# Fixing the order of TensorE's work around the first way back of a long convolution

## The chip, the cores and the metric

The kernel runs on one core of a Trainium2 chip, in float32. The metric is the device time of one execution in microseconds. A core has TensorE (PE, matmuls), VectorE (DVE), ScalarE (ACT), GpSimd (POOL) and SyncE (SP), each with its own queue that is worked off in order, and 16 DMA engines that are shared by the transfers which SP, ACT and POOL issue.

## The reference

One layer of an encoder over 1024 positions and 1024 channels: a normalised input `xn` is multiplied by one large matrix `w_in`, whose columns feed a state-space branch (S5), a long-convolution branch (Hyena), their gates and the merge. What matters here is the Hyena branch:

```python
proj = xn @ w_in[l]
u_s5, g_s5, p_hy, g_hy, m_logits = jnp.split(proj, SPLITS, axis=-1)
...
v, x1, x2 = jnp.split(sc, HY_ORDER + 1, axis=-1)      # sc: width-3 convolution of p_hy
kf = hyena_filters(L, w1, b1, freq, w2, b2, w3, decay)
z = v.astype(f32)
for o, g in enumerate((x1, x2)):
    zf = jnp.fft.rfft(z, n=2 * L, axis=1)
    conv = jnp.fft.irfft(zf * kf[:, o][None], n=2 * L, axis=1)[:, :L]
    z = g.astype(f32) * (conv + d[o].astype(f32) * z)
return z.astype(proj.dtype) * jax.nn.silu(gate)
```

So `z` goes to frequencies and back twice. The first way back is multiplied by the gate `x1`, the second by `x2` and by the SiLU of a further projection.

## The kernel before

Every product is computed with operands split in a high and a low part, in three passes (high x high, high x low, low x high). A **projection** is one call of `proj`: 128 output channels over all positions, 3 x 8 x 2 = 48 matmuls into a PSUM tile `pps` (there are two), whose rows are all L541. Its weights come in by `prefetch`, in the fixed order of `self.order`: a load by SP into `wraw` (L508, three buffers), ACT's cast to `whi` (L510) and negation into `wlo` (L511), and an adding transfer issued by POOL that leaves the residue in `wlo` (L512). There are two pairs of `whi` and `wlo` (`wp`, two buffers), so weights are at most two projections ahead.

The stages around the change, in order of the program:

- `hy_forward0`: the first way to the frequencies. Projections of v are turned and multiplied with the constants `zc` (L686, L697); DVE combines the results with the filter's spectra (L704 to L725) and ACT stores the spectra to DRAM (L761).
- `hy_inverse0`: the first **way back**, eight blocks of 128 channels. `inverse` multiplies four spectra (`yraw`, loaded by SP at L609 and split into `y` by ACT and DVE, L109 and L113) with the constants `ic` (eight loads by SP, L600, into the space that the first forward stage has left): 48 matmuls, L633 and L635. ACT and DVE join the halves (L639 to L644), POOL multiplies by the gate and writes the sums over the gate's tile (`rotate`, L821 to L825). `store` then **turns** the block by eight transposes (L671), splits it into `z1`, which has a single buffer (L673, L674), and ACT sends it to DRAM (L831). The gates come from eight projections of x1 (`use_x1`); there are five gate tiles, so the gate of x1(5) can be written only after block 0 has been turned.
- `hy_forward1`: the second way to the frequencies, like the first, from the blocks stored in DRAM. Beside it run 16 projections, in pairs gate(c) and x2(c): ACT takes the SiLU of gate(c) into the single tile `sg` (L871), and x2(c) is convolved (L563 to L566), folded with it (L589 to L591) and stored (L878).
- `tail` and `output`: the second way back (`hy_inverse1`, the same `inverse`), whose pools and constants are set up when the second forward stage is closed, then the two last matrices.

The order on each engine is fixed before the kernel runs, by a scheduler: of the instructions whose inputs are ready by its own reckoning it queues the earliest in program order. So a projection that stands later in the program is pulled forward where the PE would otherwise have nothing. `tc.issue_after(i)` sets a bound to that: whatever is traced in its block on the engine of `i` is queued behind `i`. In the kernel before there are two such places here: x2(2) stands behind the last turn, and the second forward stage behind x2(2).

Of the kernel before, what the change touches and what calls it, by code (L numbers as in the profile page):

```python
# [9 lines left out]
F = mybir.dt.float32  # L10
# [7 lines left out]
L = 1024  # L18
# [82 lines left out]
class Trunk:  # L101
# [422 lines left out]
    def proj(self, c, use, name="w_in", x=None):  # L524

        self.projs([(c, use)], name, x or (self.xh, self.xl), ())

    def projs(self, cols, name, x, cuts):

        nc = self.nc  # L530
        xh, xl = x
        nk = xh.shape[1]
        part = lambda x, kc, hf: x[kc, hf] if x is self.xl else x[:, kc, hf * 512:hf * 512 + 512]
        todo = [(self.weight((name, c, nk)), self.pp.tile([128, L], F, name="pps"), use) for c, use in cols]
        for a, b in zip((0,) + cuts, cuts + (nk,)):
            for (hi, lo), ps, _ in todo:
                for p in range(3):
                    for kc in range(a, b):
                        w, x = ((hi, xh), (hi, xl), (lo, xh))[p]
                        for hf in range(2):  # L540
                            self.summed = nc.tensor.matmul(  # L541
                                             out=ps[:, hf * 512:hf * 512 + 512], lhsT=w[:, kc], rhs=part(x, kc, hf),
                                             start=a == 0 and p == 0 and kc == 0, stop=b == nk and p == 2 and kc == nk - 1)
        for _, ps, use in todo:
            use(ps)
# [69 lines left out]
    def inverse(self, pi):  # L615

        nc = self.nc
        ps = pi.tile([128, 2, 512], F, name="iv")
        for nj, j in enumerate((0, 2, 1, 3)):
            while len(self.iv_ready) < self.iv_ahead and self.iv_todo:  # L620
                self.spectrum()
            y = self.iv_ready.pop(0)
            for par in range(2):
                for pqi in range(2):
                    cols, dst = (((slice(0, 258), ps[:, 0, 0:258]), (slice(514, 770), ps[:, 0, 256:512])),
                                 ((slice(258, 514), ps[:, 1, 0:256]),
                                  (slice(770, 1026), ps[:, 1, 256:512])))[par][pqi]
                    for a, b in ((0, 0), (0, 1), (1, 0)):
                        lhsT = y[:, a, par, pqi]
                        first = nj == 0 and pqi == 0 and a == 0 and b == 0  # L630
                        last = nj == 3 and pqi == 1 and a == 1
                        if first and par == 0:
                            nc.tensor.matmul(out=ps[:, 0], lhsT=lhsT, rhs=self.ic0, start=True, stop=False)  # L633
                        else:
                            nc.tensor.matmul(out=dst, lhsT=lhsT, rhs=self.ic[b][:, j, cols], start=first, stop=last)  # L635
        while len(self.iv_ready) < self.iv_ahead and self.iv_todo:
            self.spectrum()
        s = self.iv_w.tile([128, 2, 256], F, name="isn", bufs=1)
        nc.scalar.copy(out=s, in_=ps[:, :, 256:512])  # L639
        pm = self.iv_w.tile([128, 2, 512], F, name="pm")  # L640
        for a, op in enumerate((ALU.add, ALU.subtract)):
            nc.vector.tensor_tensor(out=pm[:, a].rearrange("p (b q) -> p b q", b=2), in0=ps[:, :, 0:256], in1=s, op=op)
        nc.vector.tensor_copy(out=pm[:, 0, 0:1], in_=ps[:, 0, 0:1])
        nc.vector.tensor_copy(out=pm[:, 1, 0:1], in_=s[:, 0, 0:1])  # L644
        return pm
# [18 lines left out]
    def to_time(self, pt, eo, z):  # L664

        nc = self.nc
        for h in range(2):
            ps = pt.tile([128, 4, 128], F, name="zt", tag="fw")
            for b in range(4):
                c = (4 * h + b) * 128  # L670
                self.turned = nc.tensor.transpose(out=ps[:, b], in_=eo[:, c:c + 128], identity=self.ident)  # L671
            hi, lo = (z[:, i, 4 * h:4 * h + 4] for i in range(2))
            nc.scalar.copy(out=hi, in_=ps)  # L673
            nc.vector.tensor_tensor(out=lo, in0=ps, in1=hi, op=ALU.subtract)  # L674
# [131 lines left out]
    def hy_inverse0(self):  # L806

        tc, nc = self.tc, self.nc
        self.d_z1 = self.dram.tile([4, 128, 2, 2048], F, name="d_z1")
        with ExitStack() as ctx:  # L810
            self.inv_pools(ctx, 0, (4, 4))
            zp = ctx.enter_context(tc.tile_pool(reuse_waits="tile", name="iv_z", bufs=1, side="right"))
            pi = ctx.enter_context(tc.tile_pool(reuse_waits="tile", name="iv_p", bufs=1, space=PSUM, side="right"))
            pt = ctx.enter_context(tc.tile_pool(reuse_waits="tile", name="iv_pt", bufs=2, space=PSUM, side="right"))
            gates, back = {}, {}
            self.inverse_start(0)

            def rotate(c):
                g = gates.pop(c)
                pm = self.inverse(pi)  # L820
                nc.gpsimd.tensor_tensor(out=pm, in0=pm, in1=g, op=ALU.mult)  # L821
                nc.gpsimd.tensor_tensor(out=g[:, 0], in0=pm[:, 0], in1=pm[:, 1], op=ALU.add)
                nc.gpsimd.tensor_tensor(out=g[:, 1], in0=pm[:, 0], in1=pm[:, 1], op=ALU.subtract)
                nc.gpsimd.tensor_copy(out=g[:, 0, 0:1], in_=pm[:, 0, 0:1])
                nc.gpsimd.tensor_scalar(out=g[:, 1, 0:1], in0=pm[:, 1, 0:1], scalar1=-1.0, scalar2=None, op0=ALU.mult)  # L825
                back[c] = g

            def store(c):
                z = zp.tile([128, 2, 8, 128], R, name="z1")
                self.to_time(pt, back.pop(c).rearrange("p a b -> p (a b)"), z)  # L830
                nc.scalar.dma_start(out=self.d_z1[c // 2][:, c % 2], in_=z.rearrange("p h a c -> p (h a c)").bitcast(F))  # L831

            for c in range(10):
                def use_x1(ps):
                    g = self.gates[c % len(self.gates)]
                    self.fold(self.conv(ps, 8 + c, "cv"), None, g)
                    gates[c] = g.rearrange("p a b c d -> p a (b c d)")

                if c < 8:
                    self.proj(16 + c, use_x1)  # L840
                if 0 < c < 9:
                    rotate(c - 1)
                if c > 1:
                    store(c - 2)

    def hy_forward1(self, tail):

# [2 lines left out]
        with self.tc.tile_pool(reuse_waits="tile", name="sg", bufs=1) as sp, self.tc.tile_pool(reuse_waits="tile", name="vf1", bufs=2) as self.vf, \  # L850
                ExitStack() as ctx:
            wp, fwd = self.fwd_pools(ctx, 1)

            def forwards():
                for cq in range(4):
                    z = wp.tile([128, 2, 2, 8, 128], R, name="z")
                    for ct in range(2):
                        nc.sync.dma_start(out=z[:, ct].rearrange("p h a c -> p (h a c)").bitcast(F),
                                          in_=self.d_z1[cq][:, ct])
                    yield  # L860
                    yield from fwd(cq, z)

            f = forwards()
            next(f)
            silu = {}

            def gate(c):
                silu[c] = sp.tile([128, L], F, name="sg")

                def use_g(ps):  # L870
                    nc.scalar.activation(out=silu[c], in_=ps, func=AF.Silu)  # L871
                self.proj(32 + c, use_g)

            def x2(c):
                def use_x2(ps):
                    t = self.vf.tile([128, 2, 2, 2, 128], F, name="vf")
                    self.fold(self.conv(ps, 16 + c, "cv"), silu.pop(c), t)
                    nc.scalar.dma_start(out=self.d_x2[c], in_=t.rearrange("p a b c d -> p (a b c d)"))  # L878
                self.proj(24 + c, use_x2)

            blocks = [(use, c) for c in range(8) for use in (gate, x2)]
            for use, c in blocks[:5]:
                use(c)
            with self.tc.issue_after(self.turned.ins):
                x2(2)
            with self.tc.issue_after(self.summed.ins):
                next(f)
            for _ in f:
                pass
            ctx.close()  # L890
            tail()
            for use, c in blocks[6:]:
                use(c)

    def exp(self, pool, out, x, shape):

# [598 lines left out]
```

## Time and profile before

| | us |
|---|---|
| median of three runs | 1426.94 (1425.91 to 1428.88) |
| profiled execution | 1429.46 |
| its span | 1427.5 |
| PE busy | 1352.0 |
| DVE busy | 1011.3 |
| ACT, POOL busy | 515.6, 385.3 |

The profile is of one execution. Its timeline names start and length of each run of like instructions, and in brackets how long the engine had been idle and what ended that. Matmul lengths overlap their successors, so the pace of a run of matmuls is read from one start to the next. The table of stretches gives each engine's busy time in it and PEclk, the clock granted to TensorE, 1.00 being 2.4 GHz and 0.50 being 1.2 GHz.

### The profile page before, as it was taken

The numbers are of one execution on the slowest core, as the hardware profiler recorded it, in microseconds if no ns is written. First come the engines' busy times: TensorE is split into PE (matmuls) and PEld (weight loads), VectorE is DVE, ScalarE is ACT, GpSimd is POOL, SyncE is SP. The second block draws the span as 40 slices with busy tenths as digits, with TensorE's granted clock in tenths as the row PEclk, the third lists the DMA queues.
The fourth block names the chain that finished last, engine by engine and source line by source line (L and its number), as shares of the span: only waits on it lengthen the run. The fifth ranks groups of instructions, "written<-read, shape, count | busy, mean of one in ns | idle before, by whom it ended". The sixth has DMA issues, their size and how long they took to land.

```text
span 1427.5 us, 19526 instructions
## 1 busy us (share of the span) xinstructions
PE 1352.0 (95%) x7219; PEld 1138.5 (80%) x7219; DVE 1011.3 (71%) x1938; ACT 515.6 (36%) x737; POOL 385.3 (27%) x331
## 2 busy tenths in 40 slices
PE   5888899999999999999999999999799998999998
PEld 3777788888887877878888888888688877978886
DVE  7999998699589887314389995455388966843632
ACT  5576664223333232333233223443222224432322
POOL 3766775000000000232122200335301112332222
PEclk9998999999999999999999999999899997999999
DMA  8221224865685554566975659765878899766431
GB/s 278 84 83 74 82 97 144 203 164 143 178 275 140 117 125 94 151 165 173 324 218 169 175 178 270 204 193 187 287 248 270 261 299 301 204 186 153 132 108 71
DMA packets 188619, 257.24 MB, mean 180 GB/s; under 512 B 23069, under 2 KB 144153, under 8 KB 185788
## 3 DMA queue, kind: packets, MB, share of 16 engines
q1 hardware_dynamic: 149212, 153.69, 34.6%
q0 software_dynamic: 11520, 39.85, 14.5%
q10 hardware_dynamic: 27792, 62.45, 12.1%
q8 instruction: 57, 0.93, 0.3%
q14 instruction: 38, 0.31, 0.1%
HBM read 147.49 MB, written 76.82 MB: 157 GB/s over the span
## 4 chain that ended last, share of the span: by engine, by line
PE 61%; DVE 15%; DMA 9%; issue 3%; SPq 1%; ACT 1%; DVEq 0%; ACTq 0%
PE pps L541 38%; PE ops L1396 6%; PE iv L635 6%; DMA d_y<-x 3%; PE po L404 2%; PE fwo L686 2%; PE pe L414 1%; DMA d_z<-z 1%; DMA wlo<-wraw 1%; DMA yraw<-d_y 1%; DMA zc<-c_zc_lo_d 1%; DVE st L1228 1%; DVE st L1226 1%; PE zt L671 1%; DVE m L722 1%
## 5 line engine op out<-in xcount | busy, mean ns | idle before, releaser
L512 POOL DMA_DIRECT2D wlo<-wraw x76 | 65.9, 867 | 683.5 <-ACT wlo L511 509.1
L541 PE MATMUL pps<-xh,whi 128*128 128x512 f32 x896 | 227.4, 402 | 9.9 <-ACT sg L871 6.7
L541 PE MATMUL pps<-xl,whi 128*128 128x512 f32 x896 | 225.0, 397 | 0.0
L541 PE MATMUL pps<-xh,wlo 128*128 128x512 f32 x896 | 221.9, 396 | 0.0
L541 PEld LDWEIGHTS pps<-xh,whi 128*128 128x128 f32 x896 | 168.3, 191 | 49.0 <-ACT sg L871 6.9
L541 PEld LDWEIGHTS pps<-xh,wlo 128*128 128x128 f32 x896 | 166.9, 188 | 39.1
L541 PEld LDWEIGHTS pps<-xl,whi 128*128 128x128 f32 x896 | 165.9, 188 | 38.0 <-issue 0.2
L510 ACT CAST whi<-wraw 128x1024 fp32r<-128x1024 f32 (+1 forms) x76 | 74.7, 983 | 286.1 <-PE pps L541 266.9
L404 PE MATMUL po<-sh,fo 128*128 128x256 f32 x512 | 100.8, 291 | 6.2 <-DVE sh L111 5.1
L113 DVE TENSOR_TENSOR y<-yraw,y 128x512 fp32r<-128x512 f32 x64 | 55.0, 873 | 71.1 <-ACT y L109 70.8
L635 PE MATMUL iv<-ic,y 128*128 128x256 f32 (+1 forms) x752 | 99.0, 290 | 5.2 <-ACT y L109 3.2
L635 PEld LDWEIGHTS iv<-ic,y 128*128 128x128 f32 x752 | 97.2, 198 | 8.0 <-ACT y L109 3.7
L404 PEld LDWEIGHTS po<-sh,fo 128*128 128x128 f32 x512 | 83.7, 196 | 9.1 <-DVE sh L111 6.1
L511 ACT ACTIVATE wlo<-whi 128x1024 fp32r<-128x1024 f32 (+1 forms) x76 | 74.9, 986 | 27.3 <-PE pps L541 25.5
L357 POOL TENSOR_TENSOR acc<-acc,sq 128x512 f32<-128x512 f32 x56 | 76.8, 1371 | 22.2 <-ACT sq L342 20.1
L404 PE MATMUL po<-sl,fo 128*128 128x256 f32 x256 | 74.0, 289 | 1.0 <-DVE sl L113 1.0
L109 ACT CAST y<-yraw 128x512 fp32r<-128x512 f32 x64 | 39.1, 621 | 62.5 <-PE iv L635 43.9
L404 PEld LDWEIGHTS po<-sl,fo 128*128 128x128 f32 x256 | 50.2, 196 | 2.1 <-DVE sl L113 1.3
L564 DVE SCALAR_TENSOR_TENSOR cv<-pps,cw,cv 128x1023 f32<-128x1023 f32 x24 | 30.7, 1278 | 28.7 <-ACT cv L563 28.7
L333 PE MATMUL g<-w3h,ha 128*128 128x512 f32 x64 | 33.6, 525 | 17.1 <-DVE e L338 16.1
L686 PE MATMUL fwo<-z,zc 128*128 128x256 f32 x384 | 49.6, 283 | 0.0
L336 ACT ACTIVATE e<-dec,negt 128x512 f32<-128x512 f32 x64 | 45.2, 716 | 11.5 <-DVE so L350 4.8
(437 smaller groups left out, 2674.6 us busy)
## 6 DMA issues: line engine op xcount, KB each, us to landing
wlo<-wraw POOLq DMA_DIRECT2D x64, 512.0 KB, 5.7
wraw<-w_in SPq DMA_DIRECT2D x56, 512.0 KB, 5.2
kspec<-ko SPq DMA_DIRECT2D x32, 512.0 KB, 3.0
kt<-kspec SPq DMA_DIRECT2D x32, 512.0 KB, 4.9
d_y<-x ACTq DMA_DIRECT2D x32, 512.0 KB, 3.6
yraw<-d_y SPq DMA_DIRECT2D x64, 256.0 KB, 5.5
d_m<-cv ACTq DMA_DIRECT2D x16, 512.0 KB, 2.7
d_z<-z ACTq DMA_DIRECT2D x8, 1024.0 KB, 4.5
```

Source lines behind the costliest of these rows:

```text
L109: nc.scalar.copy(out=hi, in_=src)
L113: e.tensor_tensor(out=lo, in0=src, in1=hi, op=ALU.subtract)
L336: nc.scalar.activation(out=e, in_=decf, func=AF.Exp, scale=negt[:, tt:tt + 1])
L357: nc.gpsimd.tensor_tensor(out=acc, in0=acc, in1=sq, op=ALU.add)
L404: nc.tensor.matmul(out=po[:, part], lhsT=fo[a][:, 12 * (jj % 2) + b], rhs=sd[4 + i][d][:, part], start=n == 0 and part == 0, stop=n == 11 ...
L510: nc.scalar.copy(out=hi, in_=raw)
L511: nc.scalar.activation(out=lo, in_=hi, func=AF.Copy, scale=-1.0)
L512: nc.gpsimd.dma_start(out=lo, in_=raw, accum_op=ALU.add)
L541: self.summed = nc.tensor.matmul(out=ps[:, hf * 512:hf * 512 + 512], lhsT=w[:, kc], rhs=part(x, kc, hf), start=a == 0 and p == 0 and kc == ...
L635: nc.tensor.matmul(out=dst, lhsT=lhsT, rhs=self.ic[b][:, j, cols], start=first, stop=last)
L686: nc.tensor.matmul(out=out, lhsT=zc[a][:, b], rhs=z[:, :, d, zi], start=start and n == 0, stop=stop and n == 3 * len(prods) - 1)
L1396: nc.tensor.matmul(out=pss[cs.start][:, 0:cs.stop - cs.start], lhsT=m[:, kc, ts], rhs=w[kc][:, cs], start=kc == 0 and p == 0, stop=kc == 7 ...
```

## The change

The x1 projections of the first way back are divided: five come whole ahead of block 0, the other three are cut into their three passes (`proj_thirds`), and one or two such thirds are put between two blocks, by the list 1, 2, 1, 1, 1, 2, 1, 0. On the PE every block is queued behind the third before it, every third behind the block before it. Only gate(0) is then bound between the last block and the second forward stage; the other 15 late projections follow in the program after the second forward stage and after `tail`, in the order x2(0), gate(1), x2(1) and on, with no bound.

```diff
+    def proj_thirds(self, c, use):
+
+        nc = self.nc
+        (hi, lo), ps = self.weight(("w_in", c, 8)), self.pp.tile([128, L], F, name="pps")
+        for p, (w, x) in enumerate(((hi, self.xh), (hi, None), (lo, self.xh))):
+            for kc in range(8):
+                for hf in range(2):
+                    cs = slice(hf * 512, hf * 512 + 512)
+                    self.summed = nc.tensor.matmul(out=ps[:, cs], lhsT=w[:, kc],
+                                                   rhs=self.xl[kc, hf] if x is None else x[:, kc, cs],
+                                                   start=p == 0 and kc == 0, stop=p == 2 and kc == 7)
+            if p == 2:
+                use(ps)
+            yield
...
-            for c in range(10):
+            def x1(c):
                 def use_x1(ps):
...
-                if c < 8:
-                    self.proj(16 + c, use_x1)
-                if 0 < c < 9:
-                    rotate(c - 1)
-                if c > 1:
-                    store(c - 2)
+                return 16 + c, use_x1
+
+            for c in range(5):
+                self.proj(*x1(c))
+            thirds = (t for c in range(5, 8) for t in self.proj_thirds(*x1(c)))
+            for c, n in enumerate((1, 2, 1, 1, 1, 2, 1, 0)):
+                with tc.issue_after(self.summed.ins):
+                    rotate(c)
+                if c:
+                    store(c - 1)
+                with tc.issue_after(self.rotated.ins):
+                    for _ in range(n):
+                        next(thirds)
+            store(7)
...
-            blocks = [(use, c) for c in range(8) for use in (gate, x2)]
-            for use, c in blocks[:5]:
-                use(c)
-            with self.tc.issue_after(self.turned.ins):
-                x2(2)
+            with self.tc.issue_after(self.rotated.ins):
+                gate(0)
             with self.tc.issue_after(self.summed.ins):
                 next(f)
             for _ in f:
                 pass
             ctx.close()
             tail()
-            for use, c in blocks[6:]:
-                use(c)
+            for c in range(8):
+                if c:
+                    gate(c)
+                x2(c)
```

`self.rotated` is the last matmul of a block, `self.summed` the last matmul of a projection or of a third.

## Rows read from the trace of the kernel before

**Rows 1.** Page, part 1: busy time, share of the span and instructions by engine

```profile
PE 1352.0 (95%) x7219; PEld 1138.5 (80%) x7219; DVE 1011.3 (71%) x1938; ACT 515.6 (36%) x737; POOL 385.3 (27%) x331
```

**Rows 2.** Busy time by stretch: length, engines' busy, granted clock, DMA share, GB/s

```profile
895.00:1006.20 111.20, 106.83 (x674) 95.01 (x673) 52.22 (x91) 44.40 (x65) 48.50 (x47) 1.00 0.70 203
...
1006.20:1025.80 19.60, 13.19 (x48) 10.59 (x49) 6.00 (x7) 3.51 (x5) 4.06 (x2) 0.74 0.95 357
...
1025.80:1175.10 149.30, 149.30 (x793) 127.24 (x791) 128.09 (x164) 35.06 (x38) 23.80 (x15) 1.00 0.81 258
...
1175.10:1250.00 74.90, 64.44 (x431) 60.08 (x431) 52.14 (x71) 34.42 (x52) 23.62 (x10) 0.89 0.87 251
```

**Rows 3.** Timeline of PE: start, length, operation, count; units, block 0, last turns

```profile
857.96 3.90 PE L541 MATMUL pps<-xh,whi 128*128 128x512 f32 x16
...
869.15 3.90 PE L541 MATMUL pps<-xh,whi 128*128 128x512 f32 x16
...
895.29 0.40 PE L633 MATMUL iv<-icp,y 128*128 128x512 f32 x1
...
995.24 1.04 PE L671 MATMUL zt<-ident,gate 128*128 128x128 f32 x8
...
1229.20 0.40 PE L633 MATMUL iv<-icp,y 128*128 128x512 f32 x1
...
1234.99 0.40 PE L633 MATMUL iv<-icp,y 128*128 128x512 f32 x1
```

**Rows 4.** Timeline of PE: waits, in brackets with what ended them

```profile
1003.98 0.66 PE L671 MATMUL zt<-ident,gate 128*128 128x128 f32 x4 [2.12 <-POOL gate L824]
...
1005.27 0.66 PE L671 MATMUL zt<-ident,gate 128*128 128x128 f32 x4 [0.63 <-POOL gate L825]
...
1012.61 5.93 PE L541 MATMUL pps<-xh,whi 128*128 128x512 f32 x16 [6.68 <-ACT sg L871]
...
1018.37 3.89 PE L541 MATMUL pps<-xl,whi 128*128 128x512 f32 x16
...
1180.36 0.80 PE L633 MATMUL iv<-icp,y 128*128 128x512 f32 x1 [5.23 <-ACT y L109]
```

**Rows 5.** Timeline of DVE, SP's queue and ACT around the first constants

```profile
867.61 1.23 DVE L720 TENSOR_TENSOR m<-x,kt 128x1024 f32<-128x1024 f32 x1
...
868.91 0.34 SPq L600 DMA_DIRECT2D ic<-c_ic_hi_d  x1
...
890.65 1.37 ACT L109 CAST y<-yraw 128x512 fp32r<-128x512 f32 x2 [1.58 <-DMA yraw<-d_y]
```

**Rows 6.** Busy time by stretch, as rows 2: the load of the constants

```profile
866.00:890.60 24.60, 24.60 (x107) 19.79 (x106) 10.34 (x13) 7.09 (x7) 1.72 (x2) 1.00 1.01 314
...
882.00:886.00 4.00, 4.00 (x19) 3.23 (x18) 2.36 (x2) 0.71 (x1) 0.86 (x1) 1.00 1.03 416
```

**Rows 7.** DMA from 866 to 892: queues with share, issues with us to landing

```profile
q1 hardware_dynamic: 4524, 6.08, 71.6%
...
q0 software_dynamic: 288, 1.05, 20.2%
...
wlo<-wraw POOLq DMA_DIRECT2D x2, 512.0 KB, 8.9
```

**Rows 8.** Timeline of POOL and ACT at the last turn

```profile
1004.01 0.92 POOL L512 DMA_DIRECT2D wlo<-wraw  x1
...
1007.99 1.07 ACT L673 CAST z<-zt 128x512 fp32r<-128x512 f32 x2 [4.98 <-DMA d_z<-z]
```

**Rows 9.** Instructions on tile zc, 980 to 1060: the low half's issue, its landing

```profile
L661 SPq DMA_DIRECT2D zc<-c_zc_lo_d x1: 320/320/320, 1006.0 to 1006.0; - x1
...
DMA to landing us min/median/max: 15.8/15.8/15.8
```

**Rows 10.** Timeline of PE and DVE: two ends of the forward stages

```profile
717.79 0.86 PE L686 MATMUL fwe<-z,zc 128*128 128x256 f32 x5 [1.32 <-DMA zc<-c_zc_lo_d]
...
1161.44 0.68 DVE L725 TENSOR_TENSOR x<-m 128x512 f32<-128x512 f32 x1
```

More of the change, by code (lines that the diff above doesn't have):

```diff
@@ L634, in inverse @@
                         else:
-                            nc.tensor.matmul(out=dst, lhsT=lhsT, rhs=self.ic[b][:, j, cols], start=first, stop=last)
+                            self.rotated = nc.tensor.matmul(out=dst, lhsT=lhsT, rhs=self.ic[b][:, j, cols], start=first, stop=last)
         while len(self.iv_ready) < self.iv_ahead and self.iv_todo:
@@ L670, in to_time @@
                 c = (4 * h + b) * 128
-                self.turned = nc.tensor.transpose(out=ps[:, b], in_=eo[:, c:c + 128], identity=self.ident)
+                nc.tensor.transpose(out=ps[:, b], in_=eo[:, c:c + 128], identity=self.ident)
             hi, lo = (z[:, i, 4 * h:4 * h + 4] for i in range(2))
```

## The prediction, made before the changed kernel ran

> **What bounds the kernel now.** I read the engine shares first: TensorE (PE) is busy for 95% of the span [rows 1]. A PE this full is helped only where it waits or where its clock has fallen, so the next view is the table of stretches from where the change begins to act [rows 2]; a stretch's length less its busy time is idle time. To see slow matmuls inside the busy time I use two units: a projection of 48 matmuls takes 11.19 us (857.96 to 869.15, 0.233 each), one block of the way back 5.79 (1229.20 to 1234.99) [rows 3]. What is lost:
>
> - 857.96 to 895.29: the PE goes on with projections without a gap, nothing lost.
> - 895.0 to 1006.2 (first way back): 111.20 less 106.83 busy, 4.4 lost. The two waits at the last turn, 2.12 and 0.63, are in it [rows 4].
> - 1006.2 to 1025.8: 19.6 for one projection, 8.4 lost: a wait of 6.68, then a slow start, sixteen matmuls in 5.76 (1012.61 to 1018.37) where 3.73 is usual [rows 4]. The granted clock is 0.74 over the stretch [rows 2], part of it at the lower of the two levels.
> - 1025.8 to 1175.1 (second forward stage): busy throughout, nothing lost; DVE has 128.09 of it.
> - 1175.1 to 1250.0 (second way back): 431 matmuls, of which eight blocks are 384. 46.3 + 47 x 0.233 = 57.3, so 17.6 lost: 10.5 idle, beginning with a wait of 5.23 [rows 4], and 7.1 of slow matmuls at a mean clock of 0.89 [rows 2].
>
> Together **30.4 us lost**. The change adds no matmul and takes none away, so its time is a matter of this ledger alone.
>
> **What the change does to the order.** Five projections of gates (x1) now run before block 0, three are cut into thirds between the blocks, and gate(0) comes behind block 7. In the trace of before the PE ends its fifth x1 at 857.96, then runs the other three and most of gate(0) until block 0 starts at 895.29 [rows 3]. That work is now barred: thirds are queued behind block 0, gate(0) behind block 7, block 0 behind x1(4). Nothing else can step in, since there are two pairs of weight tiles, filled in a fixed order, and x1(5) and x1(6) hold both.
>
> **Term 1, the gap before block 0.** Block 0 needs the constants `ic` and its first spectrum. SP issues `ic` only at 868.91, right after DVE's last product of the first forward stage (867.61 + 1.23) has freed the space [rows 5]. DVE lags behind the PE there, and this part of its queue is not touched. The first spectrum is cast at 890.65 [rows 5], behind the eight loads of `ic` (128 x 1026 floats each) and the start matrix: 21.7 us for some 4.7 MB. The DMA engines are full meanwhile (share 1.01) [rows 6], 71.6% of their time on SP's queue and 20.2% on POOL's, whose two transfers are weight residues [rows 7]. Both belong to weights whose tiles are now not free, so they go. If SP's queue takes over their time, 21.7 x 71.6 / 91.8 = 16.9 us, and with the cast block 0 starts near 887. **Gap: 29 us.** Bounds: 23, if all 4.7 MB went at the best rate within this load (416 GB/s [rows 6], 11.4 us), and 33 if nothing speeds up. I take 29, the value nearest to the row of this very load.
>
> By the Trainium skill ("DMA: Bandwidth & Descriptors", section "Where 436 GB/s comes from") HBM holds a core to about 358 GB/s; as an estimate this load would take 13.2 us, the gap would be 25 and the sum below 4 us smaller. The trace disagrees with both ends of that: 314 GB/s over the load, 416 in a part of it [rows 6].
>
> **Term 2, the restart.** After the wait of 6.68 us the first sixteen matmuls lost 2.0 [rows 4]. No row shows a longer stop here; the second way back, which stops several times, loses 7.1. One stop: I take **2**.
>
> **Term 3, the loop of eight blocks.** Between two blocks now stands one third (3.73 us) or two (7.46). A turn must wait for ACT's copy, DVE's sums and POOL: from the end of block 7 (995.24, where the turn before starts [rows 3]) it is 8.7 us to the first half at 1003.98 and 10.0 to the second at 1005.27 [rows 4]. With one third between, the next turn comes 3.73 + 5.79 + a turn of at most 1.04 later, 10.6 us: slack 0.6. What could use it up: POOL's queue holds a weight residue ahead of the turn's last element (0.92 us at 1004.01 [rows 8]); ACT's holds spectrum casts behind the copy into `z1`, a single buffer, for which it once waited 4.98 us [rows 8]; SP's holds weight loads ahead of spectra. If all fits, 0; if each of the five one-third periods loses 1.6, 8. I take **3**.
>
> **Term 4, the start of the second forward stage.** The low half of its constants `zc` is issued after the last turn, at 1006.0, and takes 15.8 us to land [rows 9]. Now block 7 ends near 978 (887 + 2 + 46.3 + six turns, 6 + nine thirds, 33.6 + 3), its turn comes 10 us later, and `zc` lands near 1004. On the PE, gate(0) and two turns last until 991. If the forward matmuls are queued right behind gate(0), 13 us idle and 2 of slow clock: 15. If x2(0) (11.2 us) goes first, being ready and not barred, about 2; if gate(1) does too, 0. In the first forward stage the first such matmuls stood 1.32 us too early for the same constants [rows 10]. I take **3**.
>
> **Term 5, what closes.** The 4.4 and 8.4 go: gate(0) covers the turn of block 7, and ACT's drain of it no longer stands behind the wait for `z1`. In the second forward stage 15 projections instead of ten are left. The stage runs at DVE's pace: 135.6 us from 1025.8 to DVE's last sum at 1161.44 [rows 10]. Starting at 1004 it ends near 1140, constants and first spectra need 22 more (as in term 1), and the PE has projections until 978 + 16 x 11.2 + 1.6 + 37.4 (the stage's own matmuls: 149.3 less 480 x 0.233) + 3 = 1199. So the 17.6 goes as well. Some can return where eight blocks run back to back and each wants four spectra: 0 to 8. I take **2**, since the late blocks of before did run so, at 5.79 [rows 3].
>
> **Sum.** Lost after: 29 + 2 + 3 + 3 + 2 = 39.0, against 30.4: **+8.6 us**. The profiled execution took 1429.46 (span 1427.5) and would become 1438; it lay 2.5 above the median of the runs shown, 1426.94. Forecast: 1426.94 + 8.6 = **1435.5 us**.
>
> **Rivals.**
> - *Fast load* (not slower): without the weight traffic the constants come at 416 GB/s, the gap is 23, and terms 3 to 5 lose 2 together: 23 + 2 + 2 = 27, time **1423.5**. It decides once gap and stalls together are below 28.4. For it: block 0 waits for DMA alone. Against: the mean of 314 GB/s in the same load [rows 6], and its spectrum stores stay.
> - *The second forward stage stands bare* (slower still): the full 15 of term 4, 29 + 2 + 3 + 15 + 2 = 51, time **1447.5**. For it: `zc` was met too early once [rows 10]. Against: x2(0) and gate(1) may go first.
> - *The gap doesn't open*, since the order that comes out isn't the one written and other work fills it: 3 + 3 + 2 = 8 lost, time **1404.5**. Against: the two pairs of weight tiles.
>
> **How the numbers follow.** Forecast (1430 to 1443) 0.54, bare forward stage (1443 to 1455) 0.16, fast load and what lies near it (1420 to 1430) 0.22, no gap 0.08. From 1422 to 1449 lies about 0.8: the forecast, most of the fast load, the bare stage up to its worked-out time. A measurement of this kernel tells some 0.2% (2.9 us) from no change. Faster by more (below 1424.1): no gap and a third of the fast load, 0.15. Within: the rest of the fast load, 0.16. Slower: 0.69.
>
> **What would show it.** Right: a PE idle from about 858 to 887 that ends on a spectrum's cast, no POOL residue between 862 and that point, a low clock in block 0, a full PE through the second forward stage, and no 5 us wait ahead of the second way back. Term 1 is wrong if block 0 starts before 881 or after 892; term 3 if waits between blocks come to over 8; term 4 if the first forward matmul waits over 5 us; term 5 if the second way back still starts at a low clock. All fails if the x1 projections are spread over the first forward stage so that the PE never runs out of work.

## The result and the profile after

| us | before | changed |
|---|---|---|
| median, runs on one chip | 1427.91 (1425.91 to 1429.64) | 1440.36 (1439.06 to 1442.31) |
| profiled execution, its span | 1429.46, 1427.5 | 1442.31, 1440.2 |
| PE busy | 1352.0 (95%) | 1347.0 (94%) |

The changed kernel takes 1.0089 times as long (95% interval 1.0069 to 1.0108), some 12.7 us more; forecast were 8.6. The PE even works 5 us less, for the same 7219 matmuls, since fewer of them run at the lower clock; what has grown is its idle time. In the table of stretches of the changed kernel (length, busy time of PE, PEld, DVE, ACT and POOL with counts, granted clock, DMA share, GB/s), the first row is the gap ahead of block 0, the second block 0, the third the other seven blocks with the thirds, the fourth gate(0) and the second forward stage, the last the rest up to the point at which the third column block of the next projection begins:

```profile
858.90:887.46 28.56, 0.16 (x2) 0.01 (x1) 12.55 (x20) 2.77 (x3) 0.86 (x1) 0.57 0.89 281
887.46:894.72 7.26, 7.26 (x49) 7.03 (x49) 3.87 (x6) 3.39 (x6) 0.00 (x0) 0.80 0.63 182
894.72:974.26 79.54, 79.54 (x530) 72.47 (x529) 51.04 (x82) 34.80 (x54) 44.15 (x38) 1.00 0.61 184
974.26:1158.96 184.70, 181.77 (x938) 152.62 (x936) 137.91 (x176) 45.90 (x50) 42.35 (x25) 1.00 0.86 271
1158.96:1275.56 116.60, 109.14 (x641) 95.42 (x641) 60.79 (x86) 47.51 (x64) 31.61 (x16) 0.99 0.76 214
```

They answer to [rows 2]. The gap is 28.6 us with an idle PE; block 0 takes 7.26 where 5.79 is usual, at a mean clock of 0.80; the seven blocks behind it fill their stretch wholly (79.54 of 79.54). The timeline of PE in the same kernel has the waits behind these rows (start, length, operation, count, and in brackets the idle time before it with what ended it). Line 536 is a third, 556 a whole projection, 648 and 650 a block:

```profile
855.16 3.90 PE L556 MATMUL pps<-xh,wlo 128*128 128x512 f32 x16
...
887.46 0.79 PE L648 MATMUL iv<-icp,y 128*128 128x512 f32 x1 [28.40 <-ACT y L109]
...
888.05 6.84 PE L650 MATMUL iv<-ic,y 128*128 128x258 f32 x47
...
894.72 3.90 PE L536 MATMUL pps<-xh,whi 128*128 128x512 f32 x16
...
974.26 3.90 PE L556 MATMUL pps<-xh,whi 128*128 128x512 f32 x16
...
1005.23 0.85 PE L701 MATMUL fwe<-z,zc 128*128 128x256 f32 x5 [0.79 <-DMA zc<-c_zc_lo_d]
...
1163.68 0.80 PE L648 MATMUL iv<-icp,y 128*128 128x512 f32 x1 [4.57 <-ACT y L109]
...
1164.49 3.35 PE L556 MATMUL pps<-xh,whi 128*128 128x512 f32 x9
...
1202.92 5.60 PE L650 MATMUL iv<-ic,y 128*128 128x258 f32 x46
...
1275.56 3.97 PE L556 MATMUL pps<-ozh,whi 128*128 128x512 f32 x16 [1.57 <-DVE ez L1378]
```

At 855.16 stands the last pass of the fifth x1, at 887.46 block 0 after 28.40 us: the place that [rows 3] shows without a gap. The wait of 6.68 us and the two at the last turn in [rows 4] have gone. The wait of 5.23 us ahead of the second way back has not: at 1163.68 it is 4.57, and it is odd, because projections follow at 1164.49 and last until 1202.92, nearly all of which were ready, as a run below bears out. The PE stood before two block matmuls that had been queued ahead of them.

The load that ended the gap, in SP's, ACT's and POOL's timelines of the changed kernel, answers to [rows 5] and [rows 7]:

```profile
869.80 0.34 SPq L615 DMA_DIRECT2D ic<-c_ic_hi_d  x1
...
886.78 0.62 ACT L109 CAST y<-yraw 128x512 fp32r<-128x512 f32 x1 [25.54 <-DMA yraw<-d_y]
...
861.53 0.86 POOL L512 DMA_DIRECT2D wlo<-wraw  x1 [10.33 <-ACT wlo L511]
```

From the first load of `ic` to the first cast of a spectrum it is 16.98 us, against 21.74 before. The residue at 861.53 is the last that POOL issues before block 0. It has landed before the load begins: in the DMA view from 866 to 892, the stretch of [rows 7] (packets, MB, share of the 16 engines), POOL's queue q0 has no row any more:

```profile
q1 hardware_dynamic: 5627, 6.63, 79.4%
q10 hardware_dynamic: 288, 1.05, 9.9%
```

### The profile page after: what moved, and what is told of

Same layout as the page of the kernel before. It is cut to its first block, busy times and chain, and to the rows that moved or that the text cites. A ratio compares the mean times of both kernels' runs of the same rounds, so it can differ in the third digit from the quotient of the medians.

```text
span 1440.2 us, 19526 instructions
## 1 busy us (share of the span) xinstructions
PE 1347.0 (94%) x7219; PEld 1133.2 (79%) x7219; DVE 1012.9 (70%) x1938; ACT 516.1 (36%) x737; POOL 398.3 (28%) x331
## 4 chain that ended last, share of the span: by engine, by line
PE 63%; DVE 15%; DMA 9%; issue 2%; ACT 1%; POOL 1%; SPq 0%; ACTq 0%; DVEq 0%; POOLq 0%
PE pps L556 38%; PE ops L1417 6%; PE iv L650 5%; DMA yraw<-d_y 3%; DMA zc<-c_zc_lo_d 2%; PE po L404 2%; PE pps L536 2%; PE fwo L701 2%; DMA d_y<-x 2%; PE pe L414 1%; PE fwe L701 1%; DVE st L1249 1%; DVE st L1247 1%; PE zt L686 1%; DMA ic<-c_ic_lo_d 1%
## 5 line engine op out<-in xcount | busy, mean ns | idle before, releaser
L556 PE MATMUL pps<-xh,whi 128*128 128x512 f32 x848 | 216.6, 403 | 4.0 <-DVE cv L581 4.0
L556 PE MATMUL pps<-xl,whi 128*128 128x512 f32 x848 | 212.5, 397 | 0.0
L556 PE MATMUL pps<-xh,wlo 128*128 128x512 f32 x848 | 210.1, 396 | 0.0
L556 PEld LDWEIGHTS pps<-xh,whi 128*128 128x128 f32 x848 | 159.9, 192 | 41.4 <-ACT wlo L511 3.6
L556 PEld LDWEIGHTS pps<-xh,wlo 128*128 128x128 f32 x848 | 157.9, 188 | 36.8
L556 PEld LDWEIGHTS pps<-xl,whi 128*128 128x128 f32 x848 | 157.3, 188 | 36.2 <-issue 0.2
L650 PEld LDWEIGHTS iv<-ic,y 128*128 128x128 f32 x752 | 93.3, 191 | 3.5 <-DVE y L113 1.6
L650 PE MATMUL iv<-ic,y 128*128 128x256 f32 (+1 forms) x752 | 94.7, 284 | 1.2 <-DVE y L113 1.0
L357 POOL TENSOR_TENSOR acc<-acc,sq 128x512 f32<-128x512 f32 x56 | 76.9, 1373 | 21.8 <-ACT sq L342 19.9
L578 ACT ACTIVATE cv<-pps,cb,cw 128x1024 f32<-128x1024 f32 x24 | 29.0, 1208 | 70.4 <-PE pps L556 50.4
```

The source lines that it names most:

```text
L357: nc.gpsimd.tensor_tensor(out=acc, in0=acc, in1=sq, op=ALU.add)
L556: self.summed = nc.tensor.matmul(out=ps[:, hf * 512:hf * 512 + 512], lhsT=w[:, kc], rhs=part(x, kc, hf), start=a == 0 and p == 0 and kc == ...
L650: self.rotated = nc.tensor.matmul(out=dst, lhsT=lhsT, rhs=self.ic[b][:, j, cols], start=first, stop=last)
```

## The experiments

The kernel before was timed beside each group of runs, with medians of 1427.98 (first four) and 1428.86 (last four). The runs of it beside the changed kernel had 1427.91, so a difference from the changed kernel's median carries up to 1 us of that. The end of the fifth x1 lies between 854.7 and 858.9 in the profiles of the kernels that begin their blocks behind it, though the change doesn't reach that far back; so stretches are compared below by their length, and differences of up to 4 us between two profiles' times are not read.

**Only the thirds.** The first way back of the changed kernel, the late projections as before:

```diff
-            with self.tc.issue_after(self.rotated.ins):
-                gate(0)
+            blocks = [(use, c) for c in range(8) for use in (gate, x2)]
+            for use, c in blocks[:5]:
+                use(c)
+            with self.tc.issue_after(self.turned.ins):
+                x2(2)
...
-            for c in range(8):
-                if c:
-                    gate(c)
-                x2(c)
+            for use, c in blocks[6:]:
+                use(c)
```

> Only the first part of the change: five x1 projections whole, thirds between the blocks, but then six of the 16 late projections ahead of the second forward stage as in the kernel before, with x2(2) bound behind the last turn. Theory: gap of 28 to 29 us and the cold block as in the changed kernel, first way back without waits, and the second way back loses its 17.6 us again: before + 30 - 4.4 - 8.4 = + 17, about 1445. Rival (the late projections are what costs): below the changed kernel, under 1438.

Measured: **1445.59 us**, ratio 1.0126 (1.0111 to 1.0141), 17.6 us above the kernel before; the sum had said 17. The timeline of PE has the gap unchanged, and the stops of the second way back as in the kernel before:

```profile
884.57 0.79 PE L648 MATMUL iv<-icp,y 128*128 128x512 f32 x1 [28.63 <-ACT y L109]
...
1194.80 0.79 PE L648 MATMUL iv<-icp,y 128*128 128x512 f32 x1 [4.50 <-ACT y L109]
...
1208.28 0.50 PE L650 MATMUL iv<-ic,y 128*128 128x258 f32 x2 [2.22 <-ACT y L109]
```

So the gap belongs to the thirds' order, and what the second way back saves in the changed kernel comes from the late projections.

**Only the late projections.** The first way back as before (`for c in range(10)`), `hy_forward1` as changed.

> Only the second part of the change: the first way back as in the kernel before (eight x1 projections whole, no bound on blocks), but gate(0) behind block 7 and 15 projections beside the second forward stage. Theory: no gap ahead of block 0 (the eighth x1 ends near 892), but seven blocks wait some 3.3 us each for the block before them to be drained, 23 us, and the clock may fall in between; the stage behind is as in the changed kernel. Together 1432 to 1445. Rival (the late projections cost the time by overloading DVE in the second forward stage): the loss is there, and the first way back shows none.

Measured: **1440.03 us**, ratio 1.0080 (1.0059 to 1.0102). The eighth x1 ends as block 0 begins, and there is no gap. But gate(0) and all behind it are barred until block 7, and nothing stands between the blocks. The timeline of PE, with blocks 1, 2 and 6:

```profile
901.13 0.76 PE L648 MATMUL iv<-icp,y 128*128 128x512 f32 x1 [3.61 <-DVE pm L659]
...
909.70 1.03 PE L686 MATMUL zt<-ident,gate 128*128 128x128 f32 x8
914.83 0.76 PE L648 MATMUL iv<-icp,y 128*128 128x512 f32 x1 [4.10 <-DVE pm L659]
...
965.22 0.76 PE L648 MATMUL iv<-icp,y 128*128 128x512 f32 x1 [2.52 <-DVE pm L658]
```

and the stretch of these seven blocks (columns as above):

```profile
901.13:982.04 80.91, 61.06 (x384) 59.24 (x385) 45.21 (x72) 25.46 (x44) 40.41 (x35) 0.79 0.51 165
```

The waits add up to 23.5 us (3.61, three of 4.10, three of 2.52), as expected, at the draining of the one PSUM tile. For the clock the expectation had no figure: block 1 takes 8.57 us from start to turn (901.13 to 909.70) where 5.79 is usual, and the mean clock over the stretch is 0.79. 61.06 us busy for seven blocks (40.5 at full pace) and six turns (0.79 each) are 15.8 more. The rival, DVE in the second forward stage, is worth 0.9 us of waits (982.04 to 1170: 187.96 us, 187.11 busy). Each half of the change alone loses time, by two different stops of the PE; they are not additive, since the thirds are the cover that the other half takes from the blocks.

**Six projections ahead of block 0.** In this run the gate of x1(5) is written over that of block 0 before block 0 uses it; the amount of work is the same.

```diff
-            for c in range(5):
+            for c in range(6):
                 self.proj(*x1(c))
-            thirds = (t for c in range(5, 8) for t in self.proj_thirds(*x1(c)))
-            for c, n in enumerate((1, 2, 1, 1, 1, 2, 1, 0)):
+            thirds = (t for c in range(6, 8) for t in self.proj_thirds(*x1(c)))
+            for c, n in enumerate((1, 1, 1, 1, 1, 1, 0, 0)):
```

> The changed kernel with six x1 projections whole ahead of block 0 instead of five; two are cut, one third behind each of blocks 0 to 5, none behind blocks 6 and 7. Theory (the loss is the 28.4 us gap ahead of block 0 and the cold block behind it): the gap shrinks by one projection, 11.2 us, to about 17; block 7 loses its cover, some 3 us. Sum: about 8 us below the changed kernel, some 1432. Rival (cutting projections into thirds, or the 15 late projections, cost the time): the gap shrinks but the time stays within 3 us of the changed kernel, since the loss shows up again behind it.

Measured: **1436.65 us**, ratio 1.0066 (1.0048 to 1.0084): 3.7 below the changed kernel's median, between the two expectations. Timeline of PE at block 0 and at block 7:

```profile
886.82 0.80 PE L648 MATMUL iv<-icp,y 128*128 128x512 f32 x1 [20.00 <-ACT y L109]
...
961.59 0.77 PE L648 MATMUL iv<-icp,y 128*128 128x512 f32 x1 [3.12 <-DVE pm L659]
...
969.96 1.04 PE L686 MATMUL zt<-ident,gate 128*128 128x128 f32 x8
```

The gap shrinks by 8.4 us only, to 20.00, and block 7, uncovered, costs more than I had said: 3.12 of wait, and 8.37 instead of 5.79 for the block. SP, ACT and POOL tell why the gap gave back less than a projection:

```profile
866.42 0.34 SPq L615 DMA_DIRECT2D ic<-c_ic_hi_d  x1
...
886.15 0.62 ACT L109 CAST y<-yraw 128x512 fp32r<-128x512 f32 x1 [17.14 <-DMA yraw<-d_y]
...
869.29 0.86 POOL L512 DMA_DIRECT2D wlo<-wraw  x1 [10.33 <-ACT wlo L511]
```

With x1(5) done, its weight tiles are free, one residue is issued at 869.29, and the load takes 19.73 us. With 16.98 (no residue) and 21.74 (two, in the kernel before) that is a row of three: each residue that runs beside the load goes with some 2.4 us more. The other profiles agree: 17.21 and 16.57 with none (only the thirds; the changed kernel with the second way back bound), 21.63 to 21.98 with two (the late projections alone and the three filled kernels).

**The gap filled.** All eight x1 projections ahead of block 0, and as thirds gate(0), x2(0) and gate(1), whose inputs depend on no block. In this first form x1(5) to x1(7) write over the gates of blocks 0 to 2.

```diff
-            for c in range(5):
+            for c in range(8):
                 self.proj(*x1(c))
-            thirds = (t for c in range(5, 8) for t in self.proj_thirds(*x1(c)))
+            thirds = (t for u in (self.gate(0), self.x2(0), self.gate(1)) for t in self.proj_thirds(*u))
...
             with self.tc.issue_after(self.rotated.ins):
-                gate(0)
+                self.proj(*self.x2(1))
...
-            for c in range(8):
-                if c:
-                    gate(c)
-                x2(c)
+            for c in range(2, 8):
+                self.proj(*self.gate(c))
+                self.proj(*self.x2(c))
```

> Both ideas with the gap filled: all eight x1 projections whole ahead of block 0, and gate(0), x2(0), gate(1) cut into the nine thirds between the blocks; x2(1) behind block 7 as cover for the last turn, 12 late projections beside the second forward stage; the tile of folded gates has one buffer instead of two, to fit. Theory: no gap (the eighth x1 ends near 892, the first spectrum is ready near 891), first way back with 0 to 3 us of waits, forward start 1 to 3, second way back 5 to 10: 8 to 15 us lost against 30 before, so 1410 to 1418. Rival (thirds or late projections cost by themselves): no better than the kernel before, 1425 or more.

Measured: **1406.21 us**, ratio 0.9849 (0.9835 to 0.9864), better than the range, which had been added up wrongly: 8 to 15 lost against 30 is 15 to 22 less than the kernel before, 1406 to 1413. In the second form the matmuls stand at the same place, and the three late gates are written after their tile has been turned (`conv` convolves the projection that is held, `fold` writes it into its gate tile):

```diff
                 def use_x1(ps):
...
+                    held[c] = ps
+                    if c < 7:
+                        conv(c)
+                    if c < 5:
+                        fold(c)
...
                 if c:
                     store(c - 1)
+                    if c < 4:
+                        fold(c + 4)
+                    if c == 1:
+                        conv(7)
```

> The gap filled as in the run before of that name, but the gates of x1(5) to x1(7) are written into their tiles only after blocks 0 to 2 have been turned (their matmuls still stand ahead of block 0). Theory (the PE's order and its lost time decide, not the place of the folds): no gap, first way back with under 3 us of waits, 1404 to 1412, some 20 us below the kernel before. Rival (the late folds hold up the loop, through two buffers of convolved projections and two PSUM tiles): waits of 2 us and more between blocks, 1415 to 1425.

Measured: **1408.85 us**, ratio **0.9855** (0.9836 to 0.9874), 20.0 us below the kernel before. Timeline of PE:

```profile
886.77 3.90 PE L556 MATMUL pps<-xh,wlo 128*128 128x512 f32 x16
...
890.50 0.48 PE L648 MATMUL iv<-icp,y 128*128 128x512 f32 x1
...
890.83 6.09 PE L650 MATMUL iv<-ic,y 128*128 128x258 f32 x47
...
925.82 0.47 PE L648 MATMUL iv<-icp,y 128*128 128x512 f32 x1 [0.61 <-DVE pm L659]
...
937.48 0.47 PE L648 MATMUL iv<-icp,y 128*128 128x512 f32 x1 [1.01 <-DVE pm L659]
...
1009.20 0.86 PE L701 MATMUL fwe<-z,zc 128*128 128x256 f32 x5 [0.47 <-DMA zc<-c_zc_lo_d]
...
1188.22 0.79 PE L648 MATMUL iv<-icp,y 128*128 128x512 f32 x1 [5.03 <-ACT y L109]
```

Block 0 follows the eighth x1 without a wait; the first way back has two waits, 0.61 and 1.01. Its stretches:

```profile
890.50:978.55 88.05, 86.32 (x577) 78.09 (x577) 61.09 (x87) 40.68 (x62) 48.88 (x40) 1.00 0.75 212
978.55:1160.00 181.45, 180.98 (x938) 153.04 (x937) 137.60 (x180) 46.08 (x52) 34.39 (x23) 1.00 0.89 282
1160.00:1240.00 80.00, 73.37 (x491) 67.76 (x490) 50.88 (x74) 34.02 (x50) 24.64 (x11) 0.96 0.86 244
```

The PE idles 1.7 us in the first way back and 0.5 in the second forward stage, where the kernel before lost 12.8 in and behind its first way back. With the gap filled, the change goes from 12 us too slow to 20 us faster, so neither thirds nor late projections cost much by themselves. The edit does more than fill the gap: other projections become the thirds, 12 instead of 15 stand late, and a tile has a buffer less. But the 31.5 us between the two medians are about what the gap and block 0 had lost, 28.4 and 1.5. The second way back still idles 6.6 us.

**The second way back bound.** The changed kernel, and then the filled one, with

```diff
-                self.hy_inverse1(zh, zl)
+                with tc.issue_after(self.summed.ins):
+                    self.hy_inverse1(zh, zl)
```

> The changed kernel with one bound more: the second way back is queued on the PE behind the last of the late projections. In the changed kernel two of its matmuls stand 3.3 projections ahead and wait 4.57 us for a spectrum. Theory (they are queued too early, and what stands behind them was ready): that wait and some 2 us of slow clock behind it go, 5 to 7 us below the changed kernel, 1434. Rival (the load of constants and spectra sets the pace of the second way back, so the wait only moves): within 2 us of the changed kernel.

Measured: **1434.65 us**, ratio 1.0046 (1.0033 to 1.0058), 5.7 below the changed kernel's median. The timeline of PE shows the last pass of the last projection and three blocks without a wait behind it:

```profile
1190.41 3.90 PE L556 MATMUL pps<-xh,wlo 128*128 128x512 f32 x16
1194.14 0.39 PE L648 MATMUL iv<-icp,y 128*128 128x512 f32 x1
...
1199.96 0.40 PE L648 MATMUL iv<-icp,y 128*128 128x512 f32 x1
...
1205.83 0.40 PE L648 MATMUL iv<-icp,y 128*128 128x512 f32 x1
...
1222.50 3.13 PE L650 MATMUL iv<-ic,y 128*128 128x258 f32 x24 [1.85 <-DVE y L113]
...
1267.75 3.96 PE L556 MATMUL pps<-ozh,whi 128*128 128x512 f32 x16 [1.12 <-DVE ez L1379]
```

One wait of 1.85 follows later, and one of 0.75. From 1194.14 to 1267.75 it is 73.6 us for eight blocks and 96 matmuls of projections (68.7 at full pace), 4.9 lost; the last stretch of the changed kernel, up to the same place, has 10.3 more than its work, as the ledger below works out. What stood behind the two matmuls was ready, and the spectra were there when they came at last; the place in the queue was wrong.

> The filled kernel with the same bound on the second way back. Theory (the bound helps only where blocks stand ahead of ready projections and wait; there 72 block matmuls stand ahead of the last third of a projection without a wait): within 2 us of the filled kernel, since only one third of a projection is left to be moved. Rival (any early block costs): 4 us or more below it.

Measured: **1408.81 us**, ratio 0.9868 (0.9852 to 0.9885), the same as without it (1408.85). The 72 matmuls of the expectation are 26 in the traces of the filled kernels; no wait stands ahead of them. There the second way back's waits are not of this kind.

**The constants twice.** The eight loads issued a second time ahead of the first way back.

```diff
-        for j in (0, 2, 1, 3):
+        for j in (0, 2, 1, 3) * (1 if self.rotated else 2):
```

> The changed kernel in which the eight loads of the way back's constants are issued a second time ahead of the first way back (the same data into the same place, not for the second). Theory (the gap lasts until these loads and the first spectrum are through, at some 360 to 400 GB/s): 4.2 MB more make the gap and the time 10.5 to 14 us longer, 1451 to 1455. Rival (the gap lasts until the spectra are stored and DVE has finished the first forward stage): the time within 3 us of the changed kernel.

Measured: **1446.47 us**, ratio 1.0127 (1.0113 to 1.0141), 6.1 above the changed kernel: longer, as the load theory has it, but by half of what I expected. The timelines of SP, ACT and PE of this kernel (a line later than in the changed one):

```profile
866.32 0.34 SPq L616 DMA_DIRECT2D ic<-c_ic_hi_d  x1
...
877.02 1.82 SPq L625 DMA_DIRECT2D yraw<-d_y  x2
...
887.05 0.32 SPq L616 DMA_DIRECT2D ic<-c_ic_lo_d  x1
...
886.19 0.62 ACT L110 CAST y<-yraw 128x512 fp32r<-128x512 f32 x1 [28.42 <-DMA yraw<-d_y]
```

```profile
886.86 0.79 PE L649 MATMUL iv<-icp,y 128*128 128x512 f32 x1 [31.28 <-ACT y L110]
...
891.43 6.76 PE L651 MATMUL iv<-ic,y 128*128 128x258 f32 x35 [1.13 <-DMA ic<-c_ic_lo_d]
898.03 2.27 PE L537 MATMUL pps<-xh,whi 128*128 128x512 f32 x9
```

The order that came out puts the first two spectra at 877.02, ahead of the last six of the doubled loads. So the first cast comes 19.9 us after the first load (16.98 in the changed kernel), and the rest of the load falls on block 0, which lasts 11.17 us (886.86 to 898.03) instead of 7.26: gap and block 0 together 42.5 against 35.7, 6.8 more. That the gap lasts as long as transfers do is borne out; a price per byte is not to be had from this run.

## Why the prediction was right, and where it was off

Its ledger against the one of the changed kernel:

| lost, us | forecast | measured | from |
|---|---|---|---|
| term 1, gap | 29 | 28.4 | wait at 887.46 |
| term 2, restart | 2 | 1.5 | block 0, 7.26 less 5.79 |
| term 3, loop | 3 | 0 | stretch from 894.72, no idle time |
| term 4, forward start | 3 | 0.8 | wait at 1005.23 |
| term 5, the rest | 2 | 10.8 | below |
| sum | 39.0 | 41.5 | |
| before | 30.4 | 30.4 | [rows 2] |

**Term 1** held in its mechanism and its size: `ic` was issued when DVE's last product had freed the space, both residues went, and the load shortened to 16.98 us where 16.9 had been worked out from the shares of the queues. The estimate by the Trainium skill ("DMA: Bandwidth & Descriptors", section "Where 436 GB/s comes from"), 13.2 us, was too short for this load, and the ceiling of 358 GB/s that the section gives to HBM isn't seen as one here: the doubled load moved 388 GB/s for 8 us (876 to 884), 3.09 of 3.11 MB on SP's queue.

The prediction's "most of gate(0)" in the trace of before is one third of it (16 matmuls from 891.55 to 895.29); no term rests on that.

**Term 2** held. **Term 3** was too high, by its slack. The residues, stores and weight loads that it feared did come in between; POOL's and PE's timelines of the changed kernel show a residue ahead of the last elements of block 4, and block 4's turn:

```profile
948.38 0.89 POOL L512 DMA_DIRECT2D wlo<-wraw  x1
...
954.60 1.04 PE L686 MATMUL zt<-ident,u 128*128 128x128 f32 x8
```

But in the order that came out most turns stand in the filler that follows the next block, not directly behind that block: 11.3 to 15.3 us behind their own block instead of 10.6, and POOL was done at least 2 us ahead of each. **Term 4** held in its mechanism: x2(0) went first, gate(1) had begun, and the PE reached `zc` 0.8 us early.

**Term 5** is the step that failed, in the sentence "So the 17.6 goes as well" and its 2 us. The work was there, as forecast: projections lasted until 1202.9, and 1199 had been worked out. But the sum took ready work as sure cover. The prediction's own signs of that are there, a wait of about 5 us ahead of the second way back and a low clock at its start. The second way back's first two matmuls stood in the PE's queue ahead of it, and a queue in order waits at its head: 4.57 us at 1163.68 and a slow clock behind it (the nine matmuls from 1164.49 took 3.19 us, 2.10 at full pace). With 2.1 us of short waits in the second forward stage (974.26 to 1158.96: 2.9 idle less the 0.8 of term 4), the last stretch makes the 10.8: 116.6 us for eight blocks (46.3) and 257 matmuls of projections (60.0), 10.3 lost, of which 1.6 is left out here: the wait at 1275.56, which the kernel before has too, behind the end of its ledger (1.54 at 1263.39). The run with the bound shows that some 5.5 of it was the queue's order: its stretch loses 5.4 less, its median is 5.7 lower. I had weighed such an early place for `zc`, a row having shown it, and not for the second way back, where [rows 4] has a wait for the same spectra, though with no projection left behind it.

That the sum came out near was partly luck: term 5 was 8.8 too low, and the other four together 6.3 too high.

The ledgers explain 11.1 of the 12.7 us between the two spans. Of the rest, 0.9 lies ahead of the change (the fifth x1 ends at 858.9 instead of 857.96) and some 0.5 behind the compared stretches; what made it is not settled, and profiles differ there by more.

The rivals: the load was faster than before, but by the residues and not by the 416 GB/s of *fast load*. The second forward stage didn't stand bare. The gap opened. The time of the filled kernel is the mirror of the last: 8 us lost had been priced there at 1404.5, and 1408.85 was measured with the gap filled by other means.

## What to carry to other kernels

Work moved off a stretch to cover a later wait leaves a hole if that stretch was itself covering something: find what the moved work hid (here a load of constants that only the end of another engine's stage could start) and price the hole first. Filler for short waits is best taken from work that depends on neither side, and the work that is a prerequisite anyway goes into the hole ahead. Ready work behind the head of an in-order queue covers nothing: where two streams share an engine, bind the one whose input comes by DMA behind the other. That pays only where ready work does stand behind the head: some 5.5 us in the changed kernel, nothing in the filled one.

## What the runs showed of the hardware

In the kernel with only the late projections the PE stopped for 2.5 to 4.1 us before each block of 5.8 us and lost by its clock two thirds of what it lost by the stops: 23.5 us of waits and 15.8 of slow matmuls, at a mean granted clock of 0.79; blocks behind waits of 3.6 to 4.1 us took 8.5 to 8.6. Single stops of 28.0 to 28.6 us cost 1.5 to 2.3 in the block behind them, in three profiles, and one of 20.0 us cost 2.5. So seven short stops were dearer than one long one of a larger sum.

A load of 4.7 MB on SP's queue took some 2.4 us longer for each weight residue beside it, an adding transfer of 512 KB issued by POOL: 16.57 to 17.21 us with none (three profiles), 19.73 with one, 21.63 to 21.98 with two (five). The kernels differ in other ways too, and no run takes out a residue alone.
